# Queries and keys parted over 128 rows and placed by DMA, with forget sums, weight splits and fillers rearranged

## The chip, the cores and the metric

The kernel runs on one core of a Trainium2 chip. The metric is the time of one execution on the device in microseconds, the median of several runs. All times below are in us unless they are marked ns.

## The reference

Two layers (`DEPTH` 2) work on 512 tokens of width 1024. Each layer is a half-weighted SwiGLU block, a token mixer and a second SwiGLU block, with a layer norm behind each. The mixer projects once with `w_in`, runs three attentions of 8 heads each over heads of 64, gates their outputs and projects back:

```python
def _token_mix(h, w_in, ...):
    q_a, kv_a, g_a, q_b, k_b, v_b, q_c, k_c, v_c, f_c = _split_cols(h @ w_in)
    o_a = _nsa(q_a, kv_a, g_a, ...)      # compressed, selected and window keys, 2 groups
    o_b = _swa_sink(q_b, k_b, v_b, ...)  # window of 128, a sink in each row, 2 groups
    o_c = _fox(q_c, k_c, v_c, f_c, b_f)  # causal, with forget gates
    g = jax.nn.sigmoid(h @ w_gate + b_gate).reshape(B, S, 3, D)
    merged = g[:, :, 0] * (o_a @ w_br_a) + g[:, :, 1] * (o_b @ w_br_b) + g[:, :, 2] * (o_c @ w_br_c)
    return merged @ w_out

def _fox(q_c, k_c, v_c, f_c, b_f):
    log_f = jax.nn.log_sigmoid((f_c + b_f).astype(jnp.float32))
    c = jnp.cumsum(log_f, axis=1).transpose(0, 2, 1)
    ...
    logits = jnp.einsum('bhqd,bhkd->bhqk', qq, k) * scale
    logits = logits + cq[..., None] - c[:, :, None, :]
```

All of it is float32.

## The kernel before

**Products in three parts.** A float32 operand of a product is parted into a high part `hi` (a copy as fp32r) and a low part `lo` (the rest), and `mm3` runs three products: data high times weight high, data low times weight high, data high times weight low. For weights `wsplit` does it: ScalarE copies `raw` to `hi`, VectorE subtracts to `lo`. It does so in two operations of 512 columns each, or in one of 1024 where the pool `more` is open, which is outside of attention.

**One program per engine.** There are no loops on the chip. TensorE, VectorE, ScalarE, GpSimd (POOL) and SyncE (SP, which issues nearly all DMAs) each run a list of instructions in order, with semaphores between them. Tiles come from pools with a fixed number of buffers; a writer waits until the last reader of a buffer is done.

**The mixer, `mix(l, ...)`.** In attention all data lie transposed, the 128 partitions holding two heads of 64. `chunk(c0, then)` projects 128 columns of `w_in`: eight pieces of three products of 512 columns each, and after the eighth `then` takes the result out of PSUM. Chunks aren't run at once. Their pieces go into the list `fill`, and `pump(n)` takes n of them out. `step(cur, prev, n)` lays the scores of one batch of heads (`s`) and the transposes of the weights of the batch before (`tr`) on TensorE, and n pieces of `fill` between them; then the products with the values (`pv`) into `po`, which ScalarE copies to `o_t`. `PUMPS` lists n for each step. So the order of TensorE is written out by hand: projections fill the places in which a softmax on ScalarE and VectorE would leave TensorE without work. `last` holds two of the n pieces back for the end of the step. What attention is left with at its end, an empty step runs.

**Queries.** `ev_q` takes a query chunk (two heads) into `qs`, whose 128 rows hold for each head the high part in 64 rows and the low part in the other 64. For each head ScalarE writes the 64 high rows (L403) and VectorE the 64 low rows (L404).

**Keys.** `ev_k` parts the keys of a chunk in the same way, two operations on each engine (L414, L415), into `kh` and `kl`, each of which then needs its 64 rows a second time in the other 64. GpSimd copies them (L420), or VectorE for the first chunk.

**Order of the first chunks.** In each layer the mixer starts with the keys of the windowed heads (`CKB`), their first query, the columns of gates and forget gates (`set_gf`, 64 rows only), their second query, and `pump(29)`; behind these come `CKV + 0` and `CKV + P` (for `zk` and `zv`, the inputs of Nsa's compression), with a query between them, and then the rest.

**Forget sums.** `set_gf` puts two things into `fill`: at place 4 `late`, which transposes the gates and runs a chain of small operations on ScalarE and VectorE that ends with `f` (L465); at place 14 `m.cum`, which multiplies `f` by a triangle of ones on TensorE (`cum`, L475) and sends the sums through DRAM into the tables `nck`, which Fox reads.

**Gates.** `gate_chunk(br)` runs column block 0 of each branch's gates as fillers. One further chunk (branch 0, block 1) is run as a filler too, and its result stays in its PSUM bank in `held` until attention is over; `gates(1)` then takes it from there and computes the other two. `ps("mm")` draws on two PSUM banks, `ps()` without a tag takes the eight banks in turn.

**Names in the rows.** `pj` is a projection, `sS`, `sF`, `sN`, `sC` are scores of the windowed heads, Fox, Nsa and its compressed keys, `ptN` and `ptC` the transposed weights of Nsa, `p` and `pc` the weights themselves, `raw` a loaded weight.

Of the kernel before, what the change touches and what calls it, by code (L numbers as in the profile page):

```python
# [18 lines left out]
P = 128  # L19
S, D, F = 512, 1024, 2816  # L20
KD, KF, NB = D // P, F // P, S // P
H, DH, NSLOT = 8, 64, 32
# [42 lines left out]
def body(tc, a, out, depth=DEPTH):  # L65
    nc = tc.nc
# [49 lines left out]
    more = K()  # L116
# [12 lines left out]
    def wsplit(raw, n=KD, step=None):  # L129
        if nx.pool:  # L130
            pl, nb = nx.pool, 4
        else:
            more.n += 1
            pl, nb = (more.pool, 2) if more.pool and more.n % 5 in (4, 0) else (wt, 3)
        hi = pl.tile([P, KD, P], F32R, name="hi", tag="hi", bufs=nb)
        lo = pl.tile([P, KD, P], F32R, name="lo", tag="lo", bufs=nb)
        step = step or (n if more.pool else 4)
        for i in range(0, n, step):
            c = slice(i, i + step)
            nc.scalar.activation(hi[:, c], raw[:, c], AF.Copy)  # L140
            nc.vector.tensor_tensor(lo[:, c], raw[:, c], hi[:, c].bitcast(F32), op=OP.subtract)  # L141
        return hi, lo
# [208 lines left out]

    def mix(l, wts, pend, done_ffn, xap, xa, nxt):
        m = K()
        PB = 14
        w_in = a["w_in"][l]
        wb = [a["w_br_a"][l], a["w_br_b"][l], a["w_br_c"][l]]

# [7 lines left out]
        op = pool("op", side="right", reuse_waits="tile")  # L365
        o_t = [[op.tile([P, S], F32, name=f"o{br}{i}") for i in range(4)] for br in range(3)]
        at = pool("at", reuse_waits="tile")
# [27 lines left out]
                    nc.scalar.activation(dst, src, AF.Copy)  # L395


        def ev_q(p):

            t = at.tile([P, 2, S], F32R, name="qs", tag="qs", bufs=3)  # L400
            for s in range(2):
                h, o = slice(64 * s, 64 * s + 64), slice(64 - 64 * s, 128 - 64 * s)
                nc.scalar.activation(t[h, s], p[h], AF.Copy, scale=0.125)  # L403
                nc.vector.scalar_tensor_tensor(t[o, s], p[h], 0.125, t[h, s].bitcast(F32), op0=OP.mult,  # L404
                                               op1=OP.subtract)
            return t

        def ev_k(p, dst, first=False):

            for s in range(2):  # L410
                h, o = slice(64 * s, 64 * s + 64), slice(64 - 64 * s, 128 - 64 * s)
                kh, kl = dst(s)
                pv = p[h].rearrange("p (a b) -> p a b", b=P)
                nc.scalar.activation(kh[h], pv, AF.Copy)  # L414
                nc.vector.tensor_tensor(kl[h], pv, kh[h].bitcast(F32), op=OP.subtract)  # L415
                for x in (kh, kl):
                    if first:
                        nc.vector.tensor_copy(x[o], x[h].bitcast(F32))
                    else:
                        nc.gpsimd.tensor_scalar(x[o], x[h].bitcast(F32), 1.0, 1.0, op0=OP.mult, op1=OP.mult)  # L420

        def ks_tile():
            return at.tile([P, 8, P], F32R, name="ks", tag="ks", bufs=8)
# [14 lines left out]
        def ev_gf(p):  # L438
            t = at.tile([P, S], F32, name="vt", tag="vt", bufs=2)
            nc.scalar.activation(t[0:64], p[0:64], AF.Copy)  # L440

            def rest():
                pt = ps("tp", "gfT", (P, NB, 64))
                for tb in range(NB):
                    nc.tensor.transpose(pt[:, tb], t[0:64, tb * P:(tb + 1) * P], ident[0:64, 0:64])
                gs = at.tile([P, NB, 32], F32, name="gs")
                nc.scalar.activation(gs, pt[:, :, 0:32], AF.Copy)
                nc.vector.tensor_tensor(gs, gs, pt[:, :, 32:64], op=OP.add)
                nc.scalar.activation(gt, gs[:, :, 0:24], AF.Tanh, scale=0.5)
                nc.vector.tensor_scalar(gt, gt, 0.5, 0.5, op0=OP.mult, op1=OP.add)  # L450
                f = at.tile([P, 7, NB, H], F32, name="f")
                x, e, d, u, lu, eq, lf = [f[:, i] for i in range(7)]
                nc.vector.tensor_tensor(x, gs[:, :, 24:32], bf[:, None, :].to_broadcast([P, NB, H]), op=OP.add)
                nc.vector.scalar_tensor_tensor(e, x, -1.0, x, op0=OP.mult, op1=OP.min)
                nc.scalar.activation(e, e, AF.Exp)
                nc.vector.tensor_scalar(u, e, 1.0, None, op0=OP.add)
                nc.scalar.activation(lu, u, AF.Ln)
                nc.vector.tensor_scalar(d, u, -1.0, None, op0=OP.add)
                nc.vector.tensor_scalar(eq, d, 0.0, None, op0=OP.is_equal)
                nc.vector.tensor_tensor(d, d, eq, op=OP.add)  # L460
                nc.vector.reciprocal(d, d)
                nc.vector.tensor_tensor(lu, lu, d, op=OP.mult)
                nc.vector.tensor_tensor(lu, lu, eq, op=OP.add)
                nc.vector.tensor_tensor(lu, lu, e, op=OP.mult)
                nc.vector.scalar_tensor_tensor(lf, x, 0.0, lu, op0=OP.min, op1=OP.subtract)  # L465

                tri = at.tile([P, P], F32, name="tri", tag="pc", bufs=6)
                nc.gpsimd.affine_select(tri, ones.to_broadcast([P, P]), pattern=[[1, P]], compare_op=OP.is_ge,
                                        fill=0.0, base=0, channel_multiplier=-1)

                def cum():
                    pc = ps("tp", "cum")
                    for tb in range(NB):
                        c = tb * P
                        nc.tensor.matmul(pc[0:H, c:c + P], lf[:, tb], tri, start=tb == 0, stop=tb == NB - 1,  # L475
                                         skip_group_check=True)
# [113 lines left out]
        class Swa:  # L590
            br, nseg, ngrp = 1, 1, 1
# [53 lines left out]
        class Fox:  # L645
            br, nseg, ngrp = 2, 2, 2
# [4 lines left out]
            def s(u):  # L651
# [2 lines left out]
                kh, kl = m.kc[u.m]  # L654
                u.p = []
                st = small([P, 4, 2], "stF")
                for s in range(2):
                    p = p_tile([P, S])
                    u.p.append(p)
                    sc = ps("sc", "sF")  # L660
                    q = u.q[:, s, u.qb * P:(u.qb + 1) * P]
# [32 lines left out]
        class Nsa:  # L694
# [6 lines left out]
            def s(u):  # L701
# [21 lines left out]
                for s in range(2):  # L723
                    nc.scalar.activation(pc[:, s], pc[:, s], AF.Exp, scale=-1.0, bias=nm[:, 3 * s:3 * s + 1],
                                         accum_out=sm[:, 3 * s:3 * s + 1])
                u.p, u.n = [], []
                for s in range(2):
                    if s:
                        yield
                    pn = p_tile([P, 2, 2, P])[:, 0:near]  # L730
                    pf = p_tile([P, 2, 2, P])[:, 0:far] if far else None
                    u.p.append([pf[:, j] for j in range(far)] + [pn[:, j] for j in range(near)])
                    q = u.q[:, s, qb * P:(qb + 1) * P]
# [160 lines left out]

        def set_kb(p):
            m.kb = (ks_tile(), ks_tile())
            ev_k(p, lambda s: tuple(x[:, 4 * s:4 * s + 4] for x in m.kb), True)

        def set_gf(p):
            rest = ev_gf(p)  # L900

            def late():
                m.cum = rest()
            fill.insert(min(4, len(fill)), late)
            fill.insert(min(14, len(fill)), lambda: m.cum())


        chunk(CKB, set_kb)
# [4 lines left out]
        chunk(CKV + 0, lambda p: setattr(m, "zk", ev_z(p, 0)))  # L913
        chunk(CQB + 2 * P, set_q(m.qb, 2))
        chunk(CKV + P, lambda p: setattr(m, "zv", ev_z(p, 1)))
        cv, parts, tr = conv([a["cmp_k_w1"][l], a["cmp_v_w1"][l]])
        n0 = len(fill)
        chunk(CQB + 3 * P, set_q(m.qb, 3))
# [21 lines left out]
        held = []  # L940
# [6 lines left out]

        for br in range(3):
            gate_chunk(br)
        chunk(P, held.append, a["w_gate"][l])  # L950

        def need(u):
            if u.br == 1:
# [53 lines left out]
                for j, u in enumerate(prev):  # L1007
                    nc.scalar.activation(o_t[u.br][u.m][:, u.qb * P:(u.qb + 1) * P], po[:, j], AF.Copy)

        PUMPS = [11] * 8 + [10, 10, 12] * 4 + [8]  # L1010
        for cur, prev, n in zip(batches + [[]], [[]] + batches, PUMPS):
            step(cur, prev, n)
        while fill:
# [22 lines left out]
        def gates(d):  # L1036
            g_t = []
            for br in range(3):
                if d == 1 and br == 0:
                    p = held[0]  # L1040
                else:
                    p = ps(name="gate")
                    proj(p, wcols(a["w_gate"][l], br * D + d * P))
                t = tp_.tile([P, S], F32, name="t", tag="t", bufs=4)
                gate_ev(t, p, br, d)
                g_t.append(t)
            return g_t
# [163 lines left out]
```

## Time and profile before

| | |
|---|---|
| median of 3 runs | 2587.04 us (2584.88, 2587.04, 2588.99) |
| profiled execution | 2589.08 us, of which the span of the profile is 2587.4 |
| mean granted clock of TensorE | 0.996 |
| DMA | 256.39 MB, 99 GB/s in the mean |
| attention of layer 0, of layer 1 | about 415 to 714, 1697 to 1996 of the span |

The profiled execution is one more run, recorded by the hardware profiler; times within it are counted from the start of its span. Rows of groups give source line, engine, operation, tile out<-in, shape and count, then busy time and mean duration in ns, then the engine's idle time just before them with what ended most of it. Rows of waits give the waiting engine and tile, what released it, and sum, count and longest of the waits. Rows of the timeline give start, busy time, engine, line, operation, shape and count.

### The profile page before, as it was taken

The numbers are of one execution on the slowest core, as the hardware profiler recorded it, in microseconds if no ns is written. First come the engines' busy times: TensorE is split into PE (matmuls) and PEld (weight loads), VectorE is DVE, ScalarE is ACT, GpSimd is POOL, SyncE is SP. The second block draws the span as 40 slices with busy tenths as digits, with TensorE's granted clock in tenths as the row PEclk, the third lists the DMA queues.
The fourth block names the chain that finished last, engine by engine and source line by source line (L and its number), as shares of the span: only waits on it lengthen the run. The fifth ranks groups of instructions, "written<-read, shape, count | busy, mean of one in ns | idle before, by whom it ended". The sixth has DMA issues, their size and how long they took to land.

```text
span 2587.4 us, 34084 instructions
## 1 busy us (share of the span) xinstructions
PE 2558.4 (99%) x13099; PEld 2110.0 (82%) x13099; DVE 1212.7 (47%) x2633; ACT 960.9 (37%) x2015; POOL 210.9 (8%) x419
## 2 busy tenths in 40 slices
PE   9999999999999999999999999999999999999998
PEld 8888887788888888888888888877888888888887
DVE  4444244677654354442344432556766434533323
ACT  3222223577733232222232221345777323322211
POOL 0000000244300000000000000002432000000000
PEclk9999999999999999999999999999999999999999
DMA  6333333421143433333333332424221534233331
GB/s 214 110 96 98 98 92 102 138 73 52 46 140 89 125 107 96 95 96 96 114 90 95 96 96 97 127 71 138 62 59 34 151 98 142 83 98 98 98 91 64
DMA packets 360835, 256.39 MB, mean 99 GB/s; under 512 B 15336, under 2 KB 341032, under 8 KB 360672
## 3 DMA queue, kind: packets, MB, share of 16 engines
q1 hardware_dynamic: 359520, 250.02, 32.7%
q0 software_dynamic: 1152, 4.19, 0.4%
q8 instruction: 103, 1.69, 0.3%
q14 instruction: 60, 0.49, 0.1%
HBM read 247.83 MB, written 9.49 MB: 99 GB/s over the span
## 4 chain that ended last, share of the span: by engine, by line
PE 93%; DVE 4%; ACT 2%; issue 1%; DMA 0%; POOL 0%; POOLq 0%; DVEq 0%; ACTq 0%
PE acc L176 7%; PE acc L174 7%; PE acc L175 7%; PE pg L161 6%; PE pg L163 6%; PE pg L162 6%; PE pu L163 6%; PE pu L162 6%; PE pu L161 6%; PE pj L161 4%; PE pj L163 4%; PE pj L162 4%; PE gate L161 3%; PE gate L163 3%; PE gate L162 3%; PE brp L161 2%
## 5 line engine op out<-in xcount | busy, mean ns | idle before, releaser
L141 DVE TENSOR_TENSOR lo<-raw,hi 128x1024 fp32r<-128x1024 f32 (+2 forms) x470 | 500.9, 1074 | 853.5 <-ACT hi L140 852.3
L140 ACT ACTIVATE hi<-raw 128x1024 fp32r<-128x1024 f32 (+2 forms) x470 | 430.6, 930 | 1224.7 <-issue 707.3
L161 PE MATMUL pj<-xh,hi 128*128 128x512 f32 (+1 forms) x704 | 265.1, 377 | 0.8 <-DVE qs L404 0.7
L161 PE MATMUL pg<-xh,hi 128*128 128x512 f32 x640 | 249.9, 390 | 0.0
L163 PE MATMUL pj<-xh,lo 128*128 128x512 f32 (+1 forms) x704 | 249.4, 354 | 0.3 <-DVE lo L141 0.3
L162 PE MATMUL pj<-xl,hi 128*128 128x512 f32 (+1 forms) x704 | 248.7, 353 | 0.9 <-DVE xl L221 0.9
L162 PE MATMUL pg<-xl,hi 128*128 128x512 f32 x640 | 249.5, 390 | 0.0
L163 PE MATMUL pg<-xh,lo 128*128 128x512 f32 x640 | 249.5, 390 | 0.0
L163 PE MATMUL pu<-xh,lo 128*128 128x512 f32 x640 | 249.0, 389 | 0.0
L161 PE MATMUL pu<-xh,hi 128*128 128x512 f32 x640 | 249.0, 389 | 0.0
L162 PE MATMUL pu<-xl,hi 128*128 128x512 f32 x640 | 249.0, 389 | 0.0
L174 PE MATMUL acc<-hi,ha 128*128 128x512 f32 x576 | 227.3, 395 | 0.0
L175 PE MATMUL acc<-hi,ha 128*128 128x512 f32 x576 | 227.3, 395 | 0.0
L176 PE MATMUL acc<-lo,ha 128*128 128x512 f32 x576 | 227.2, 395 | 0.0
L203 POOL TENSOR_SCALAR st<-st 128x1 f32<-128x1 f32 x24 | 6.3, 264 | 1903.1 <-ACT junk L201 1903.1
L286 DVE TENSOR_TENSOR t<-t,pu 128x512 f32<-128x512 f32 x80 | 55.0, 687 | 216.6 <-PE pu L163 216.6
L161 PEld LDWEIGHTS pj<-xh,hi 128*128 128x128 f32 x704 | 134.0, 190 | 21.3 <-issue 7.2
L163 PEld LDWEIGHTS pj<-xh,lo 128*128 128x128 f32 x704 | 133.0, 189 | 19.8 <-DVE lo L141 0.5
L162 PEld LDWEIGHTS pj<-xl,hi 128*128 128x128 f32 x704 | 133.8, 190 | 11.5 <-DVE xl L221 1.6
L162 PEld LDWEIGHTS pg<-xl,hi 128*128 128x128 f32 x640 | 120.6, 188 | 25.1
L161 PEld LDWEIGHTS pg<-xh,hi 128*128 128x128 f32 x640 | 120.5, 188 | 25.1
L163 PEld LDWEIGHTS pg<-xh,lo 128*128 128x128 f32 x640 | 120.5, 188 | 25.0
(243 smaller groups left out, 4417.6 us busy)
## 6 DMA issues: line engine op xcount, KB each, us to landing
raw<-in_ffn_w_dram SPq DMA_DIRECT2D x264, 512.0 KB, 3.8
raw<-in_w_in_dram SPq DMA_DIRECT2D x56, 512.0 KB, 4.1
raw<-in_w_gate_dram SPq DMA_DIRECT2D x48, 512.0 KB, 4.0
raw<-in_w_out_dram SPq DMA_DIRECT2D x16, 512.0 KB, 3.5
x_sp<-xa POOLq DMA_DIRECT2D x8, 512.0 KB, 6.6
tab<-bvec SPq DMA_DIRECT2D x16, 256.0 KB, 2.8
raw<-in_cmp_k_w_dram SPq DMA_DIRECT2D x16, 256.0 KB, 2.7
raw<-in_cmp_v_w_dram SPq DMA_DIRECT2D x16, 256.0 KB, 3.3
```

The source lines that it names most:

```text
L140: nc.scalar.activation(hi[:, c], raw[:, c], AF.Copy)
L141: nc.vector.tensor_tensor(lo[:, c], raw[:, c], hi[:, c].bitcast(F32), op=OP.subtract)
L161: nc.tensor.matmul(o, hi[:, k], vh, start=first, stop=False)
L162: nc.tensor.matmul(o, hi[:, k], vl, start=False, stop=False)
L163: nc.tensor.matmul(o, lo[:, k], vh, start=False, stop=last)
L174: nc.tensor.matmul(o, sh(k)[:, t], hi[:, c], start=k == 0, stop=False)
L175: nc.tensor.matmul(o, sl(k)[:, t], hi[:, c], start=False, stop=False)
L176: nc.tensor.matmul(o, sh(k)[:, t], lo[:, c], start=False, stop=k == nk - 1)
L203: nc.gpsimd.tensor_scalar(st[:, 4:5], st[:, 3:4], 1.0 / D, EPS / ALPHA ** 2, op0=OP.mult, op1=OP.add)
L286: nc.vector.tensor_tensor(t, t, pu, op=OP.mult)
```

## The change

- `wsplit` parts a weight in one operation on each engine everywhere.
- A new `hi_lo` parts all 128 rows of a query or key chunk in one operation on ScalarE and one on VectorE, into two tiles `hl`. `ev_q` then places the four blocks of 64 rows in `qs` by four DMAs, `ev_k` the eight blocks (each part twice) in `kh` and `kl` by eight DMAs, all issued by SP. GpSimd's copies go.
- `m.cum` is appended to `fill` behind the chunk `CKV + P`.
- Two gate chunks are held instead of one. `PUMPS` deals the pieces in another way: 11 x 5, 12 x 3, then 11, 10, 11 four times, then 8.
- Some tiles share buffers: `p` has 13 instead of 14, the forget gates' scratch comes from the same buffers, and small pairs of `p` tiles become one.

```diff
-        step = step or (n if more.pool else 4)
+        step = step or n
...
-        PB = 14
+        PB = 13
...
+        def hi_lo(p, scale):
+            hi, lo = [at.tile([P, S], F32R, name="hl", tag="hl", bufs=2) for _ in range(2)]
+            nc.scalar.activation(hi, p, AF.Copy, scale=scale)
+            nc.vector.scalar_tensor_tensor(lo, p, scale, hi.bitcast(F32), op0=OP.mult, op1=OP.subtract)
+            return hi, lo
         def ev_q(p):
             t = at.tile([P, 2, S], F32R, name="qs", tag="qs", bufs=3)
-            for s in range(2):
-                h, o = slice(64 * s, 64 * s + 64), slice(64 - 64 * s, 128 - 64 * s)
-                nc.scalar.activation(t[h, s], p[h], AF.Copy, scale=0.125)
-                nc.vector.scalar_tensor_tensor(t[o, s], p[h], 0.125, t[h, s].bitcast(F32), op0=OP.mult,
-                                               op1=OP.subtract)
+            for o, x in zip((slice(0, 64), slice(64, P)), hi_lo(p, 0.125)):
+                for s in range(2):
+                    nc.sync.dma_start(t[o, s].bitcast(F32), x[64 * s:64 * s + 64].bitcast(F32))
             return t
-        def ev_k(p, dst, first=False):
-            for s in range(2):
-                ...
-                nc.scalar.activation(kh[h], pv, AF.Copy)
-                nc.vector.tensor_tensor(kl[h], pv, kh[h].bitcast(F32), op=OP.subtract)
-                for x in (kh, kl):
-                    if first:
-                        nc.vector.tensor_copy(x[o], x[h].bitcast(F32))
-                    else:
-                        nc.gpsimd.tensor_scalar(x[o], x[h].bitcast(F32), 1.0, 1.0, op0=OP.mult, op1=OP.mult)
+        def ev_k(p, dst):
+            for i, x in enumerate(hi_lo(p, 1.0)):
+                for s in range(2):
+                    k = dst(s)[i]
+                    v = x[64 * s:64 * s + 64].bitcast(F32).rearrange("p (a b) -> p a b", b=P)
+                    for o in (slice(0, 64), slice(64, P)):
+                        nc.sync.dma_start(k[o].bitcast(F32), v)
...
-            fill.insert(min(14, len(fill)), lambda: m.cum())
...
         chunk(CKV + P, lambda p: setattr(m, "zv", ev_z(p, 1)))
+        fill.append(lambda: m.cum())
...
-        chunk(P, held.append, a["w_gate"][l])
+        for br in range(2):
+            chunk(br * D + P, held.append, a["w_gate"][l])
...
-        PUMPS = [11] * 8 + [10, 10, 12] * 4 + [8]
+        PUMPS = [11] * 5 + [12] * 3 + [11, 10, 11] * 4 + [8]
...
-                if d == 1 and br == 0:
-                    p = held[0]
+                if d == 1 and br < 2:
+                    p = held[br]
```

More of the change, by code (lines that the diff above doesn't have):

```diff
@@ L395, in ev_pt @@
                     nc.scalar.activation(dst, src, AF.Copy)
+        def hi_lo(p, scale):
[3 more added lines that the diff above has]
+            return hi, lo
         def ev_q(p):
             t = at.tile([P, 2, S], F32R, name="qs", tag="qs", bufs=3)
-            for s in range(2):
-                h, o = slice(64 * s, 64 * s + 64), slice(64 - 64 * s, 128 - 64 * s)
-                nc.scalar.activation(t[h, s], p[h], AF.Copy, scale=0.125)
-                nc.vector.scalar_tensor_tensor(t[o, s], p[h], 0.125, t[h, s].bitcast(F32), op0=OP.mult,
-                                               op1=OP.subtract)
-            return t
-        def ev_k(p, dst, first=False):
-            for s in range(2):
-                h, o = slice(64 * s, 64 * s + 64), slice(64 - 64 * s, 128 - 64 * s)
-                kh, kl = dst(s)
-                pv = p[h].rearrange("p (a b) -> p a b", b=P)
-                nc.scalar.activation(kh[h], pv, AF.Copy)
-                nc.vector.tensor_tensor(kl[h], pv, kh[h].bitcast(F32), op=OP.subtract)
-                for x in (kh, kl):
-                    if first:
-                        nc.vector.tensor_copy(x[o], x[h].bitcast(F32))
-                    else:
-                        nc.gpsimd.tensor_scalar(x[o], x[h].bitcast(F32), 1.0, 1.0, op0=OP.mult, op1=OP.mult)
+            for o, x in zip((slice(0, 64), slice(64, P)), hi_lo(p, 0.125)):
+                for s in range(2):
+                    nc.sync.dma_start(t[o, s].bitcast(F32), x[64 * s:64 * s + 64].bitcast(F32))
+            return t
+        def ev_k(p, dst):
[5 more added lines that the diff above has]
+                        nc.sync.dma_start(k[o].bitcast(F32), v)
         def ks_tile():
@@ L445, in rest @@
                     nc.tensor.transpose(pt[:, tb], t[0:64, tb * P:(tb + 1) * P], ident[0:64, 0:64])
-                gs = at.tile([P, NB, 32], F32, name="gs")
+                w = at.tile([P, 11, NB, H], F32, name="gl", tag="p", bufs=PB)
+                gs = w[:, 0:4].rearrange("p a b h -> p (a b h)").rearrange("p (b c) -> p b c", b=NB)
                 nc.scalar.activation(gs, pt[:, :, 0:32], AF.Copy)
@@ L450, in rest @@
                 nc.vector.tensor_scalar(gt, gt, 0.5, 0.5, op0=OP.mult, op1=OP.add)
-                f = at.tile([P, 7, NB, H], F32, name="f")
-                x, e, d, u, lu, eq, lf = [f[:, i] for i in range(7)]
+                x, e, d, u, lu, eq, lf = [w[:, 4 + i] for i in range(7)]
                 nc.vector.tensor_tensor(x, gs[:, :, 24:32], bf[:, None, :].to_broadcast([P, NB, H]), op=OP.add)
@@ L656, in s @@
                 st = small([P, 4, 2], "stF")
+                both = p_tile([P, 2, 256]) if nk <= 256 else None
                 for s in range(2):
-                    p = p_tile([P, S])
+                    p = both[:, s] if both is not None else p_tile([P, S])
                     u.p.append(p)
@@ L726, in s @@
                 u.p, u.n = [], []
+                both = p_tile([P, 2, 2, P]) if near == 1 else None
                 for s in range(2):
@@ L729, in s @@
                         yield
-                    pn = p_tile([P, 2, 2, P])[:, 0:near]
+                    pn = both[:, s:s + 1] if near == 1 else p_tile([P, 2, 2, P])
                     pf = p_tile([P, 2, 2, P])[:, 0:far] if far else None
@@ L896, in set_kb @@
             m.kb = (ks_tile(), ks_tile())
-            ev_k(p, lambda s: tuple(x[:, 4 * s:4 * s + 4] for x in m.kb), True)
+            ev_k(p, lambda s: tuple(x[:, 4 * s:4 * s + 4] for x in m.kb))
         def set_gf(p):
```

## The prediction

> **What bounds the kernel now.** First the page, then TensorE's waits, then its instructions where the waits are.
>
> ```profile
> span 2587.4 us, 34084 instructions
> PE 2558.4 (99%) x13099; PEld 2110.0 (82%) x13099; DVE 1212.7 (47%) x2633; ACT 960.9 (37%) x2015; POOL 210.9 (8%) x419
> ```
>
> TensorE is busy for 2558.4 of 2587.4 us, and no edit takes a product from it. So all that there is to win lies in 29 us of idle time, and in time in which it is busy at less than its clock. The waits say where the idle time is:
>
> ```profile
> PE cum L475 <- DVE f L465: 7.2, 2, 3.6
> PE xT L1154 <- DMA xa<-in_x_dram: 5.0, 1, 5.0
> PE ptN L783 <- ACT p L395: 1.3, 2, 0.7
> PE ptN L783 <- DVE p L393: 1.2, 2, 0.6
> PE ptC L789 <- ACT p L395: 1.2, 2, 0.6
> PE ptC L789 <- DVE p L393: 1.0, 2, 0.5
> PE ptN L783 <- DVE pc L393: 0.7, 2, 0.3
> PE pj L161 <- DVE qs L404: 0.7, 2, 0.3
> ```
>
> The columns are the sum, the number and the longest. The largest is the forget sums (`cum`), once in each layer. Here it is in layer 0 and in layer 1, on TensorE alone (start, busy time, line, operation, count, and in brackets the wait before it):
>
> ```profile
> 435.13 0.59 PE L475 MATMUL cum<-tri,f 128*8 128x128 f32 x2 [3.60 <-DVE f L465]
> 439.48 0.80 PE L161 MATMUL pj<-xh,hi 128*128 128x512 f32 x1
> 441.20 0.40 PE L162 MATMUL pj<-xl,hi 128*128 128x512 f32 x1
> 441.44 0.39 PE L163 MATMUL pj<-xh,lo 128*128 128x512 f32 x1
> ```
>
> ```profile
> 1717.39 0.42 PE L475 MATMUL cum<-tri,f 128*8 128x128 f32 x2 [3.60 <-DVE f L465]
> 1721.33 0.50 PE L161 MATMUL pj<-xh,hi 128*128 128x512 f32 x1
> 1721.67 0.39 PE L162 MATMUL pj<-xl,hi 128*128 128x512 f32 x1
> ```
>
> And by windows, a quiet one and the two of the sums (busy us of PE and of the other engines, then granted clock, DMA share and GB/s):
>
> ```profile
> 418.00:420.00 2.00, 2.00 (x10) 1.64 (x10) 1.44 (x3) 0.00 (x0) 0.00 (x0) 1.00 0.88 249
> 435.10:439.40 4.30, 4.27 (x14) 1.71 (x14) 1.37 (x4) 1.39 (x6) 0.57 (x1) 0.50 0.34 118
> 1717.40:1721.30 3.90, 3.90 (x14) 1.63 (x14) 1.37 (x4) 1.36 (x5) 0.57 (x1) 0.56 0.37 125
> ```
>
> After 3.60 us without work the sums run at a granted clock of 0.50 and 0.56, and the projections behind them start at it too. The wait costs more than its idle time.
>
> The Trainium skill ("TensorE: Matmul & The Clock Gate", section "HAM oscillation — how this bites in real kernels") says that gaps of TensorE beyond about 3.4 us let the clock fall to half. The two gaps of 3.60 us agree.
>
> **The sums placed later (a gain).** They move behind the projection chunk that feeds `zv`, three chunks further; their input `f` is done at the moment where TensorE stops waiting, 435.1, so it is long there. Layer 0: 3.60 us idle; the sums take 439.48 − 435.13 = 4.35 us at 0.50, so 2.2 at full clock, a saving of 2.2; the next four products take 441.20 − 439.48 = 1.72 where four at the later spacing (441.44 − 441.20 = 0.24) take 0.9, a saving of 0.8. That is 6.6. Layer 1: 3.60; 1721.33 − 1717.39 = 3.94 at 0.56 against 2.2, a saving of 1.7; the first product's 0.34 instead of 0.24, 0.1. That is 5.4. Together **−12.0 us**. What reads the sums, the table for Fox, is first used some 80 us later, so nothing is late behind them. The softmax of the first windowed heads, which the gap sheltered, has seven fill pieces before its transposes in the new order.
>
> **Queries and keys (off the path in their arithmetic, on it in their landing).** The costs of the operations, by their groups in the attention of layer 0:
>
> ```profile
> L403 ACT ACTIVATE qs<-pj 64x512 fp32r<-64x512 f32 x24 | 14.1, 588 | 8.7 <-DVE qs L404 7.1 <-PE pj L163 1.4
> L427 ACT ACTIVATE vt<-pj 128x512 f32<-128x512 f32 x3 | 1.7, 579 | 0.0
> L404 DVE SCALAR_TENSOR_TENSOR qs<-pj,qs 64x512 fp32r<-64x512 f32 x24 | 16.5, 688 | 5.5 <-ACT qs L403 5.1
> ```
>
> An operation over 128 rows (579 ns) takes what one over 64 does (588), so each of 12 query and 7 key chunks of a layer loses one ScalarE and one VectorE operation: 19 x 0.588 = 11 and 19 x 0.688 = 13 us a layer, and GpSimd its copies of keys. None of them bounds (DVE 47% busy, ACT 37%), so this is worth nothing by itself; what it frees is the PSUM bank, one pair of operations earlier, and with it the 0.7 us of `pj` on `qs`: **−0.7**.
>
> In their place come 4 DMAs for each query chunk and 8 for each key chunk, 104 a layer, of 128 KB, all on SP's queue, in order with the weight loads. No DMA from SBUF to SBUF is in this trace; the nearest:
>
> ```profile
> raw<-in_w_in_dram SPq DMA_DIRECT2D x56, 512.0 KB, 4.1
> raw<-in_cmp_k_w_dram SPq DMA_DIRECT2D x16, 256.0 KB, 2.7
> raw<-in_cmp_v_w_dram SPq DMA_DIRECT2D x16, 256.0 KB, 3.3
> x_sp<-xa POOLq DMA_DIRECT2D x8, 512.0 KB, 6.6
> ```
>
> ```profile
> 433.67 0.37 SPq L518 DMA_DIRECT2D raw<-in_cmp_k_w_dram  x1
> 434.09 0.46 SPq L518 DMA_DIRECT2D raw<-in_cmp_v_w_dram  x1
> ```
>
> So SP issues one every 0.42 us, 44 us of a layer's 300, and a small load lands 2.7 us after its issue; 6.6 is the far end. Keys, and the queries of Fox and of the later windowed heads, are read 12 us or more after their chunk by the order of TensorE's instructions, so these hide it. Two kinds do not.
>
> The first query chunk, read 7 us after its end:
>
> ```profile
> 420.08 0.40 PE L158 MATMUL pj<-xh,hi 128*64 128x512 f32 x1
> 420.10 1.16 ACT L140 ACTIVATE hi<-raw 128x512 fp32r<-128x512 f32 x2 [2.31 <-PE pj L162]
> 427.60 0.66 PE L607 MATMUL sS<-ks,qs 128*128 128x128 f32 x4
> ```
>
> (Without its wait on `qs`, 0.3 in the waits above, the last row is 427.2.) ScalarE first splits a weight (until 421.2), then the query (0.588, 421.8); VectorE follows with the weight (an estimate: as long as ScalarE's 1.16, 422.4) and the query (0.688, 423.1). SP's order there is: eight key DMAs, two of the query's high part, two weight loads, two of the low part. At 0.42 each from 421.8 the weights go out at 422.6 and 423.1 and the last low part at 423.9. Alone it lands 2.7 later, 426.6: no wait. Served strictly behind the weights it is: the first weight at 422.6 + 4.1 = 426.7, the second 2.1 later (512 KB at the 249 GB/s of the first window), the low part's 256 KB 1.05 later, 429.8: a wait of 2.6. I take the middle, 1.3 a layer: **+2.6**, ends 0 and 5.2.
>
> The Trainium skill ("DMA: Bandwidth & Descriptors", section "Queues, rings and completion order") says that each DMA engine takes the descriptors of one ring in order; by that alone this term would be its upper end, 5.2, and the whole sum 2.6 us worse. The trace leans that way (the second of a pair of 256 KB loads takes 3.3 against 2.7).
>
> The four query chunks of Nsa, read soon after their end:
>
> ```profile
> 521.95 0.57 ACT L403 ACTIVATE qs<-pj 64x512 fp32r<-64x512 f32 x1
> 523.08 0.37 SPq L147 DMA_DIRECT2D raw<-in_w_in_dram  x1
> 526.48 0.30 PE L714 MATMUL sC<-kc,qs 128*128 128x64 f32 x2
> ```
>
> From the chunk's end to the read are 4.4 us in this one (526.48 less 521.95, and ScalarE starts at once). By the order of instructions 1.0 us of products more lie between them in the new kernel, and 1.8, 3.1 and 2.4 at the other three: 5.4 us of room at the tightest, and 4.4 + 2.1 = 6.5 in the mean (an estimate that gives all four this one's room). The second low part is issued about 2.4 us after the chunk's end: 0.6 for ScalarE, some 0.7 in VectorE's queue, 0.7 for its operation, 0.4 on SP. Landing after 2.7 it is there at 5.1, in time; behind a weight load issued at the same moment, as at 523.08, it lands as late as that one, in 4.1, 1.4 later, and the tightest waits 1.1. I take 0.8 a layer, **+1.6**; ends 0 and 5 (0.6 for each of the eight).
>
> SP's order also puts four query DMAs between the loads of the compression weights, whose buffers turn over in a few us: 0.3 a layer, **+0.6**, ends 0 and 2.
>
> **Weights split in one operation.** The pair of half splits takes 1.16 us on ScalarE (420.10 above); as one operation its first half comes up to 0.6 later and its second no later. A chunk's weights are made two chunks ahead; no wait of the list above is on `hi` or `lo`. Nothing, unless another operation comes to wait 0.5 us longer behind one on VectorE: inside the next term.
>
> **Fillers and the held gate.** In the last step eight projection pieces now stand between the transposes, where before two did:
>
> ```profile
> 709.18 0.30 PE L789 MATMUL ptC<-ident,pc 128*128 128x128 f32 x1 [0.49 <-DVE p L393]
> 710.42 0.66 PE L783 MATMUL ptN<-ident,p 128*128 128x128 f32 x4 [0.33 <-DVE pc L393]
> 713.99 0.50 PE L161 MATMUL gate<-xh,hi 128*128 128x512 f32 x1
> 714.14 0.45 ACT L1008 ACTIVATE o<-po 128x128 f32<-128x128 f32 x2 [2.38 <-PE po L802]
> 714.47 0.69 ACT L943 ACTIVATE t<-pj,bgate 128x512 f32<-128x512 f32 x1
> ```
>
> Those two waits go in both layers: **−1.6**. But a new one comes. Both `mm` banks are now held, and the next gate takes the bank of the first: in layer 0 its first product waits for ScalarE's copies of `po` and the tanh behind them, from 713.99 until 714.47 + 0.69 = 715.2: 1.2. One call fewer in the ring of banks makes it the bank of `po` in layer 1: 0.6. **+1.8.** Of the other waits of `ptN` and `ptC` (5.4 in the rows above, less 1.6: 3.8) more products lie ahead of some and VectorE has 10% less to do; I take half, **−1.9**, ends 0 and −3.8.
>
> **The sum.** −12.0 − 0.7 + 2.6 + 1.6 + 0.6 − 1.6 + 1.8 − 1.9 = **−9.6 us**; the ends give −16.3 and −0.3. The profiled execution took 2589.08 (its span and 1.7 around it), so 2579.5; the median of the runs lies 2.0 below it, 2587.04, so **2577**.
>
> **Rivals.** *Slower: the placed halves land late.* It stands against the change that no such DMA is in the trace, that x_sp takes 6.6 us, and that DMAs of 128 KB need the whole of SP's turn; for it that 256 KB loads land in 2.7. With landing L the first scores wait 423.9 + L − 427.2 = L − 3.3 a layer, the four Nsa queries, with room of 6.5 and 2.4 until the issue, L − 4.1 each. All else sums to −13.8, 6.9 a layer, so it decides from 5L − 19.7 = 6.9: L = 5.3. At the far row, 6.6, it is 2 x (3.3 + 10.0) − 13.8 = +12.8: 2600. Chance 0.14.
>
> *No change: the gap comes back at the first scores.* If the low part of the first query lands 3.4 us late in both layers, TensorE idles as long as before and the clock falls: 3.5 + 2.4 a layer instead of 1.3, +9.2 over the forecast: 2586. It needs the queue above and a further 0.8 us, as from VectorE being busy. Chance 0.12.
>
> *The remaining idle time goes too*: all fillers fit, nothing waits on a DMA: 2587 − 16.3 = 2571. Chance 0.12. The forecast itself has 0.62.
>
> **How the numbers follow.** About 0.2%, 5.2 us, is what a measurement of this kernel can tell from no change. The forecast is over that in nine cases of ten, the third rival always, the second seldom: faster 0.69, same 0.16, slower 0.15. The range leaves out the rest of the first rival and the far end of the third: 2569 to 2591, which is the first rival up to L = 5.7.
>
> **What would show it.** Right: no wait of `cum`; granted clock 1.0 through the attention of both layers; `cum` in about 2.2 us; waits of `sS` on the DMA of `qs` of 0 to 2.6 us, twice; a wait of `gate` on ScalarE of about 1.2 in layer 0; an idle sum of about 22 us. Wrong: a wait of `sC` on `qs` of over 1 us each, `qs` DMAs landing after 4.7 us, or a stretch at clock 0.5 behind the first scores.

## The result, and the profile after

The changed kernel takes 2600.47 us (median of 4 runs, 2596.84 to 2601.57) against 2586.96 for the kernel before: 1.005 times as long, 95% interval 1.0032 to 1.0067. Faster was forecast, 2577 in a range of 2569 to 2591; it is slower by 13.5 us, what the first rival priced at 2600.

The profiled execution took 2601.57, its span 2599.9, 12.5 more than before. The page, busy times first:

```profile
span 2599.9 us, 34236 instructions
PE 2561.5 (99%) x13099; PEld 2112.6 (81%) x13099; DVE 1175.3 (45%) x2529; ACT 933.8 (36%) x1923; POOL 177.6 (7%) x371
```

DVE, ACT and POOL lose 37, 27 and 33 us of work, as the change means them to. TensorE's idle time rises from 29.0 to 38.4, and the same products keep it busy 3.1 us longer. The waits of TensorE (sum, number, longest) say where:

```profile
PE sC L715 <- DMA qs<-hl: 6.6, 6, 1.8
PE sS L607 <- DMA qs<-hl: 4.2, 2, 3.9
PE kv L560 <- DMA cw2k<-in_cmp_k_w_dram: 4.2, 2, 2.2
PE sS L607 <- issue: 2.7, 1, 2.7
PE ptC L791 <- ACT p L395: 1.5, 2, 0.7
PE sC L715 <- DVE stF L675: 1.4, 1, 1.4
PE gate L161 <- ACT t L945: 1.1, 1, 1.1
PE gate L161 <- ACT o L1011: 0.5, 1, 0.5
```

The waits of `cum` and of `pj` on `qs` are gone, those of `ptN` and `ptC` shrink from 5.4 to 1.5. In their place stand the scores of the windowed heads (`sS`, 6.9 in all) and of Nsa's compressed keys (`sC`, 8.0), both on the placed queries, and `kv`, the second product of the compression, on its weights (4.2). Two of these rows don't name the placed queries (`sS` on issue, `sC` on `stF`); they are counted to them for their place and because they disappear when all placing goes back to the engines (below).

The sums themselves went as planned. By windows (PE's busy time, then the other engines, granted clock, DMA share, GB/s), the sums of layer 0 and layer 1 in their new place:

```profile
457.00:460.50 3.50, 3.50 (x22) 2.00 (x21) 1.88 (x6) 1.67 (x6) 0.00 (x0) 1.00 0.29 60
1747.00:1750.50 3.50, 3.50 (x22) 2.05 (x21) 1.88 (x6) 1.67 (x6) 0.00 (x0) 1.00 0.21 68
```

No gap, and full clock. But a gap of the same length opened at the first scores of layer 0. TensorE there, and SP's issues ahead of it (start and time on the queue):

```profile
431.04 1.06 PE L607 MATMUL sS<-ks,qs 128*128 128x128 f32 x4 [3.90 <-DMA qs<-hl]
431.90 0.73 PE L161 MATMUL pj<-xh,hi 128*128 128x512 f32 x1
432.43 0.63 PE L162 MATMUL pj<-xl,hi 128*128 128x512 f32 x1
```

```profile
416.07 5.01 SPq L420 DMA_DIRECT2D ks<-hl  x8
421.59 1.10 SPq L410 DMA_DIRECT2D qs<-hl  x2
422.74 1.34 SPq L147 DMA_DIRECT2D raw<-in_w_in_dram  x2
424.18 1.47 SPq L410 DMA_DIRECT2D qs<-hl  x2
426.68 0.37 SPq L518 DMA_DIRECT2D raw<-in_cmp_k_w_dram  x1
427.10 0.46 SPq L518 DMA_DIRECT2D raw<-in_cmp_v_w_dram  x1
```

The order is the predicted one: eight key DMAs, high parts, two weights, low parts. The eight keys hold SP for 5.01 us, 0.63 each. The low parts go out at 424.18 and 425.06 and land 6.73 and 6.37 us later by their records, at 430.91 and 431.43; `sS` starts at 431.04 with the first of its four. What lies between is a full set of DMA engines:

```profile
427.00:428.00 1.00, 0.14 (x3) 0.01 (x1) 0.47 (x2) 0.47 (x2) 0.00 (x0) 1.00 1.15 295
429.00:430.00 1.00, 0.00 (x0) 0.00 (x0) 0.00 (x0) 0.99 (x2) 0.00 (x0) 1.00 1.07 252
431.00:435.30 4.30, 4.15 (x12) 3.33 (x13) 2.27 (x16) 1.30 (x6) 0.76 (x2) 0.60 0.02 6
1721.93:1725.35 3.42, 3.42 (x10) 2.65 (x10) 2.27 (x16) 1.34 (x6) 0.76 (x2) 0.50 0.02 7
```

The busy share of the 16 DMA engines reads above 1 while the low parts are on their way. And behind the gap the clock falls to half: the product at 432.43 takes 0.63 us where one at full clock takes 0.39, and the granted clock is 0.60 in the mean over 4.3 us. Layer 1 shows the same (last row): `sS` starts after a gap of 2.75 us, and 1.1 us later the clock goes to half for 3.4 us.

To add both kinds of loss, I took for each product the time to the next start beyond the usual one for its number of columns (the median of the kernel before), and summed it by place, over both layers:

| place | before | after | forecast of the difference |
|---|---|---|---|
| forget sums | 13.5 | 1.7 | −12.0 |
| first scores, `sS` | 0 | 11.0 | +2.6 |
| scores of Nsa's queries, `sC` | 0 | 12.9 | +1.6 |
| compression, `kv` | 0 | 7.9 | 0 (its loads +0.6) |
| first gate behind attention | 0 | 2.2 | +1.8 |
| whole kernel | 14.6 | 27.2 | −9.6 |

The whole differs by 12.6, as the spans do. What the rows of the table leave out (transposes, `pj`, and small differences in the usual spacing) is −9.6 by difference; that this is also the number of the forecast is chance. Of the 31.8 us of `sS`, `sC` and `kv`, some 7.6 lie in five stretches at half clock, the rest is idle time.

### The profile page after: what moved, and what is told of

Same layout as the page of the kernel before. It is cut to its first block, busy times and chain, and to the rows that moved or that the text cites. A ratio compares the mean times of both kernels' runs of the same rounds, so it can differ in the third digit from the quotient of the medians.

```text
span 2599.9 us, 34236 instructions
## 1 busy us (share of the span) xinstructions
PE 2561.5 (99%) x13099; PEld 2112.6 (81%) x13099; DVE 1175.3 (45%) x2529; ACT 933.8 (36%) x1923; POOL 177.6 (7%) x371
## 5 line engine op out<-in xcount | busy, mean ns | idle before, releaser
L141 DVE TENSOR_TENSOR lo<-raw,hi 128x1024 fp32r<-128x1024 f32 (+2 forms) x414 | 490.6, 1189 | 867.4 <-ACT hi L140 867.3
L140 ACT ACTIVATE hi<-raw 128x1024 fp32r<-128x1024 f32 (+2 forms) x414 | 424.4, 1031 | 1247.0 <-issue 709.2
L161 PE MATMUL pj<-xh,hi 128*128 128x512 f32 (+1 forms) x720 | 274.8, 382 | 0.1
L163 PE MATMUL pj<-xh,lo 128*128 128x512 f32 (+1 forms) x720 | 257.5, 358 | 1.1 <-DVE lo L141 0.9
L162 PE MATMUL pj<-xl,hi 128*128 128x512 f32 (+1 forms) x720 | 256.6, 356 | 1.3 <-DVE xl L221 1.3
L161 PEld LDWEIGHTS pj<-xh,hi 128*128 128x128 f32 x720 | 137.8, 191 | 19.1 <-issue 6.6
L161 PEld LDWEIGHTS pu<-xh,hi 128*128 128x128 f32 x640 | 120.2, 188 | 25.0
```

Source lines behind the costliest of these rows:

```text
L161: nc.tensor.matmul(o, hi[:, k], vh, start=first, stop=False)
L162: nc.tensor.matmul(o, hi[:, k], vl, start=False, stop=False)
L163: nc.tensor.matmul(o, lo[:, k], vh, start=False, stop=last)
```

## The experiments

All times are medians; ratios are to the kernel before on the same chip, with 95% intervals.

**All placing back on the engines.** `ev_q` and `ev_k` as before, everything else changed.

```diff
-        def hi_lo, ev_q, ev_k ...      # shortened: by DMA
+        def ev_q, ev_k ...             # shortened: as in the kernel before
```

> The changed kernel with its queries and keys parted and placed as before (64 rows at a time on ScalarE and VectorE, second copies of keys by GpSimd); all else of the change stays. Theory A (the placed halves land late): the waits of sS on qs (11.0 us with the half clock behind them), of sC on qs (12.9) and of kv on the compression weights behind the key DMAs (7.9) go, 31.8 in all; pj on qs (1.2) comes back: 2600.5 - 30.6 = 2570. Theory B (the arrangement of fillers and held gates costs it, and the waits on qs only stand where others would): the transposes and the first scores wait for the softmax instead, and it stays at 2587 or above. In A TensorE's idle sum is about 20 us, in B 30 or more.

2572.50 us, 0.9945 (0.9933 to 0.9958). Theory A holds: the placing costs the changed kernel 28 us (forecast 30.6), and everything else of the change gains 14. Its waits:

```profile
PE ptC L791 <- ACT p L395: 1.5, 2, 0.7
PE pj L161 <- ACT vt L440: 1.4, 2, 0.7
PE pj L163 <- DVE lo L141: 1.1, 2, 0.8
PE gate L161 <- ACT t L945: 1.1, 1, 1.1
```

No `sS`, `sC` or `kv` is left, and the transposes wait about as long as in the changed kernel (`ptC` 1.5 in both, `ptF` 1.1 against 0.4), which speaks against theory B. TensorE's idle sum is 20.5 us, as theory A had it.

**Queries alone and keys alone by DMA.** Each is the changed kernel with one of the two functions of before.

> The changed kernel with its keys as before, its queries still by DMA. Theory A, by parts: the wait of kv goes (7.9 us with the clock), since the eight key DMAs ahead of the compression weights are gone; the waits of sC stay (12.9) and that of sS mostly (the weight loads still stand ahead of the low half): 2592, between 2588 and 2594. If the number of DMAs on SP's queue is what makes all of them late (104 a layer become 48), the waits on qs shrink too, and it is 2580 or below.

> The changed kernel with its queries as before, its keys still by DMA. Theory A, by parts: the waits of sS and sC on qs go (23.9 us), pj on qs comes back (1.2), the wait of kv stays (7.9): 2578, between 2575 and 2582. If the keys' DMAs are themselves late for scores, sS, sF or sN wait on ks instead, and it is above 2585.

With the keys on the engines: 2582.20, 0.9984 (0.9976 to 0.9993). With the queries on the engines: 2573.09, 0.9947 (0.9935 to 0.9960). Both forecasts by parts are too high, by 10 and 5 us: the parts don't add, and the first run comes near the other reading, by the number of DMAs on SP's queue (2580 or below), without reaching it. Against 2572.5, queries alone by DMA cost 9.7, keys alone 0.6, both 28. The rows of the first:

```profile
PE sC L720 <- DMA qs<-hl: 2.9, 7, 1.1
PE sS L612 <- DMA qs<-hl: 2.7, 2, 1.5
PE sC L720 <- DVE stF L680: 1.1, 1, 1.1
```

and of the second:

```profile
PE kv L562 <- DMA cw2k<-in_cmp_k_w_dram: 2.3, 2, 1.2
```

So no product waits for a placed key (no such row in any run). The keys' DMAs are harmful by what they do to others: to the queries and to the compression's weights.

**Which keys.** The changed kernel with the first chunk's keys, or Nsa's two chunks, on the engines.

```diff
-            ev_k(p, lambda s: tuple(x[:, 4 * s:4 * s + 4] for x in m.kb))
+            ev_k_of_before(p, lambda s: ..., True)      # first chunk; in the other run nsa_k's call
```

> The changed kernel with only the keys of the first chunk as before (their eight DMAs in each layer gone); all other keys and all queries by DMA. Theory A: those eight DMAs, 5.0 us of SP's time right ahead, push the two weight loads behind them into the path of the first query's low half. Without them the low half lands as in the kernel with all keys on the engines (idle 2.7 us in both layers instead of 6.7, without a clock at half): 11.0 us become some 3, and it is 2600.5 - 8 = 2592.5. Rival: the low half is late because it follows weight loads on its queue however early they are: sS keeps 10 us or more, 2600.

> The changed kernel with only Nsa's two key chunks as before (sixteen DMAs of a layer gone). Theory A: the compression weights are issued and land in time, kv's wait goes with the clock at half behind it (7.9), and the first of Nsa's queries, right behind the second chunk's eight DMAs, waits less (4.3 us in both layers with the clock): 2600.5 - 7.9 - 1 to 3 = 2590 to 2592. Rival: kv waits for weights that are late for another reason (the Fox keys' DMAs, which stand ahead of them too): 2597 or above.

First chunk: 2587.43, 1.0005 (0.9996 to 1.0014). Nsa's: 2593.34, 1.0031 (1.0021 to 1.0042). The rows of the two:

```profile
PE sS L621 <- DMA qs<-hl: 2.6, 2, 1.6
PE kv L574 <- DMA cw2k<-in_cmp_k_w_dram: 4.2, 2, 3.2
PE sC L729 <- DMA qs<-hl: 3.3, 3, 1.5
```

```profile
PE sS L621 <- DMA qs<-hl: 4.1, 2, 3.9
PE kv L574 <- DMA cw2k<-in_cmp_k_w_dram: 3.1, 2, 1.8
PE sC L729 <- DMA qs<-hl: 4.5, 7, 2.0
```

Without the eight first DMAs, `sS` waits 2.6 instead of 6.9 and the clock stays at 1.00 there. One of the two weight loads now goes out at 416.6, long before the query. The other still goes out right ahead of the low parts, at 422.76, and these land 4.8 and 4.4 us after their issue instead of 6.7 and 6.4. By windows:

```profile
415.00:435.00 20.00, 18.41 (x87) 14.19 (x86) 12.03 (x36) 10.26 (x20) 0.71 (x2) 1.00 0.41 105
```

In the changed kernel this stretch reads 15.99 us busy, clock 0.92 and a share of 0.65. The rival (late however early the loads are) falls. The run gained 13.0, not 8: `sC` waits less too, and why the first chunk's keys touch that is not shown. Nsa's keys gained 7.1 by the median (its runs lie between 2591.4 and 2600.4) where 9 to 11 were forecast; `kv` still waits 3.1 instead of 4.2, so Nsa's own key DMAs are only part of its cause, as its rival said.

**Other queues.** The changed kernel with the placing DMAs issued by another engine.

```diff
-                    nc.sync.dma_start(t[o, s].bitcast(F32), ...)      # and in ev_k
+                    nc.scalar.dma_start(...)                          # or nc.gpsimd
```

> The changed kernel with all its placing DMAs issued by ScalarE, on ScalarE's own DMA queue, instead of by SP between the weight loads. Theory A (what makes the halves late is that they stand in one queue behind weight loads, and that SP is issuing for 89 us of a layer's 300): a half lands in about 2.3 us, as the key DMAs with no load ahead of them do, the waits of sS, sC and kv on DMAs shrink from 17 us of idle time to under 5; ScalarE takes over some 60 us of issuing a layer and waits for VectorE's low parts, so that some transposes come to wait for the softmax: 2575 to 2590. Theory B (SBUF to SBUF transfers share the DMA engines with the weights and are slow beside them, whatever the queue): the low halves land in 4.5 to 6.7 us still and it stays at 2595 or above.

> The changed kernel with its placing DMAs issued by GpSimd. The transfers from GpSimd's queue in the traces (x_sp) land 5.3 to 6.6 us after their issue. Theory A: the halves are off SP's queue, so kv's wait goes (7.9 with the clock), but a landing of 5 us or more makes the waits of sS and sC as long as they are: 2590 to 2605. If the halves land in under 3 us from this queue too, the waits go and it is 2575 to 2580.

ScalarE: 2600.19, 1.0051 (1.0035 to 1.0066). GpSimd: 2631.86, 1.0176 (1.0162 to 1.0190). Theory A failed in both: ScalarE's time is where theory B put it (2595 or above), GpSimd's lies 27 us above the upper end of its range. The groups of DMAs (KB each, median us to landing), of the changed kernel and then of ScalarE's queue:

```profile
ks<-hl SPq DMA_DIRECT2D x112, 128.0 KB, 2.5
qs<-hl SPq DMA_DIRECT2D x96, 128.0 KB, 3.2
raw<-in_w_in_dram SPq DMA_DIRECT2D x56, 512.0 KB, 4.3
```

```profile
ks<-hl ACTq DMA_DIRECT2D x112, 128.0 KB, 4.6
qs<-hl ACTq DMA_DIRECT2D x96, 128.0 KB, 3.5
```

A queue of their own doesn't make them faster. Sorting the placed halves whose landing is recorded by whether SP issued a weight load (256 or 512 KB) in the 2 us ahead (median us to landing, number):

| kernel | none ahead | one or more ahead |
|---|---|---|
| changed, queries on SP | 2.7 (21) | 4.5 (9), 6.7 (1 with two ahead) |
| queries on ScalarE's queue | 3.0 (21) | 4.6 (6), 4.9 (2) |
| queries on GpSimd's queue | 2.7 (55) | 4.7 (27), 4.2 (14) |
| keys on ScalarE's queue | 4.2 (18) | 5.2 (10) |
| keys on GpSimd's queue | 3.8 (69) | 5.1 (43) |

A half with one weight load just ahead lands 1.0 to 2.1 us later, on every queue, though the loads stand on SP's. The bytes count: behind two loads of 512 KB a half took 6.7 us on SP (6.8 and 7.0 in two other runs) and 6.9 on GpSimd's queue, one record each; most of the 4.2 on GpSimd's are behind two of 256 KB. So the delay goes with the loads and not with the queue in which the half stands, which points to the DMA engines, read as full above. No run changed their load alone. The Trainium skill ("DMA: Bandwidth & Descriptors", section "Queues, rings and completion order") says of the first two that SP's and ScalarE's queues are rings on the same engines and not engines of their own; this table agrees. On ScalarE the issuing disturbs its own order besides: its operation for the next query, behind eight key DMAs, sat idle for them,

```profile
423.35 0.60 ACT L401 ACTIVATE hl<-pj 128x512 fp32r<-128x512 f32 x1 [7.58 <-DMA ks<-hl]
```

since the two `hl` buffers were still being read. There `sS` no longer waits on `qs`, but TensorE waits for a PSUM bank that VectorE's part of `hl` still reads (3.6), at `sC` (6.1) and at `kv` (6.4): the time is that of the changed kernel, the waits are others. On GpSimd `sC` alone waits 21.4 us: GpSimd issues in order and idles ahead of the placing DMAs for ScalarE's part (91.5 us in all) and VectorE's (19.1), with its scaling of weights behind them.

**The sums alone.** The kernel before with `m.cum` moved.

> The kernel before with nothing but the forget sums moved behind the chunk for zv. The prediction's first term alone: the 3.6 us gap and the half clock behind it go in both layers, 2587 - 12 = 2575 (2574 to 2577), granted clock 1.0 there. Rival: the first scores' softmax, sheltered by the gap before, is now waited for at its transposes (ptS), up to 3.6 us a layer: 2582 or above.

2575.92, 0.9961 (0.9947 to 0.9974), 10.3 us less. The first term of the prediction was right; no `ptS` waits.

**The placing alone.** The kernel before with `ev_q` and `ev_k` by DMA.

```diff
-        PB = 14
+        PB = 12                        # and hi_lo, ev_q, ev_k of the changed kernel
```

> The kernel before with nothing but the placing by DMA (and two buffers fewer for p, to have the room). Theory A: the waits of sC and kv add (12.9 + 7.9); that of sS stands ahead of the forget sums, whose chain goes on meanwhile, so the two overlap and the larger is paid (11.0 for 13.5): 2586 + 20.8 = 2607, between 2603 and 2610. If they do not overlap, all of the 28 us that the placing costs in the changed kernel come on top: 2614.

2624.44 (2616.86 to 2628.16), 1.0143 (1.0127 to 1.0158): more than either theory gave. The profile is that of the fastest run. It shows the overlap that theory A expected, for only one of `sS` and `cum` is waited for,

```profile
PE sC L714 <- DMA qs<-hl: 10.4, 9, 2.3
PE kv L560 <- DMA cw2k<-in_cmp_k_w_dram: 7.8, 2, 3.9
PE sS L607 <- DMA qs<-hl: 6.8, 3, 4.1
```

and `sC` and `kv` wait longer than in the changed kernel (8.0 and 4.2). Whether the two buffers fewer for `p` or the other order of fillers does that wasn't separated.

**Fillers and gates.** The kernel with all placing on the engines, once with one held gate and the fillers of before, once with the third gate of block 1 in a bank of the scores.

```diff
-                    p = ps(name="gate")
+                    p = ps("sc" if d == 1 else None, name="gate")
```

> The changed kernel with queries and keys parted and placed as before, one held gate and the fillers dealt as before: what is left of the change is the late sums, the weights split in one operation and the shared buffers. If these two are worth nothing, it has the time of the late sums alone, 2576, and the 3.4 us between that and 2572.5 belong to the fillers and the second held gate; if the weight splits in one operation are what ended the waits of ptN and ptC (some 7 us of them are gone), it is 2572 to 2573.

> The changed kernel with queries and keys parted and placed as before, and the third gate of column block 1 taking a PSUM bank of the scores instead of the bank of the first held gate. The first gate products behind attention then wait for nothing: without the 1.1 and 0.5 us of idle time (2.2 with the clock) it is 2572.5 - 2 = 2570 to 2571. If another wait of the same end (the table load of the tanh, po) stands behind it, 2572.

Old fillers: 2577.53, 0.9968 (0.9955 to 0.9980). So the new dealing and the second held gate are worth 5.0 us, and weights split in one operation with the shared buffers nothing that can be told (2577.5 against 2575.9 of the sums alone, intervals overlapping). The other bank: 2571.28, 0.9939 (0.9927 to 0.9952), 1.2 us less; the intervals don't tell the two apart, but no `gate` row is left.

**What can be kept of the placing.** Queries on the engines, keys by DMA, the compression's second weights loaded with the step ahead of Nsa's keys, and the gate's bank.

```diff
             def tr():
+                wk, wv = ...; nc.sync.dma_start(wk[:, :, r], v); nc.sync.dma_start(wv, ...)
                 pt = ps("tp", "glT", (P, 2, P))
```

> The changed kernel with queries as before and keys by DMA, the compression's second weights loaded one step earlier, ahead of Nsa's key DMAs, and the third gate of block 1 in a bank of the scores. Without kv's wait (2.3 us of idle time) and the gates' (1.2 by the run with the other bank) it is 2573.1 - 3.5 = 2569.5; if the GpSimd copies and second operations that the key DMAs replace are worth anything, it is below the version with all on the engines and the gate's bank (2571.3), otherwise within 1 us of it.

2566.01 (2565.44 to 2568.88), 0.9923 (0.9909 to 0.9936): by its median faster than every other version here. Its largest waits inside attention:

```profile
PE ptC L795 <- ACT p L395: 1.5, 2, 0.7
PE pj L161 <- ACT vt L442: 1.4, 2, 0.7
```

`kv` is gone by loading 192 KB a step earlier. The median is 5.3 us below the version with all placing on the engines and the gate's bank, with intervals that just overlap. Part of it is chance: in the profiled execution of that version the clock is at half for 3.4 us from 41.0 on, ahead of everything in which the two differ, and in this one it is not (this run first):

```profile
38.00:46.00 8.00, 8.00 (x37) 5.74 (x37) 4.26 (x8) 1.62 (x3) 0.00 (x0) 1.00 0.61 171
38.00:46.00 8.00, 8.00 (x31) 5.57 (x31) 4.18 (x8) 1.35 (x2) 0.00 (x0) 0.79 0.56 159
```

By the start of the 301st product this run is 1.9 us ahead (49.3 against 51.2); what follows is 3.2 us shorter. With nothing late behind them, the keys' DMAs seem to bring that much; by what is not shown.

## Why the prediction was wrong, point by point

**Right.** The bound: TensorE's idle time and its clock, nothing else. The late sums: −12.0 forecast, −11.8 by the table and −10.3 as an edit alone (medians). `cum` takes 2.3 us from first start to next product (457.36 to 459.63 in the timeline), 2.2 forecast. The held gate: +1.8 forecast, 1.6 of idle time. `pj` on `qs`: gone. Transposes: −3.5 forecast, 5.4 to 1.5, −3.9. Parting over 128 rows and weights in one operation are worth nothing by themselves. All this is the 14 us that the kernel gains without the placing.

**Wrong: the landing of the placed queries.** This is the step that failed, and three sizes were off in it. SP's issue was taken as 0.42 us from loads from DRAM; a placing DMA holds SP for 0.59 in the median (`ks` 461 to 1391 ns, `qs` 461 to 1636). The last low half was to go out at 423.9 and went at 425.06. Its landing was taken as the middle between 2.7 and "behind the weights"; it was beyond the end, 431.43 against 429.8; two further loads of 256 KB, which the estimate left out, went out meanwhile (426.68 and 427.10); whether they delayed it is not shown. And each gap was priced at its idle time alone, though the first part of the prediction had just shown that a gap of 3.6 us costs the clock too. Together: first scores +11.0 for +2.6 (end 5.2), Nsa's queries +12.9 for +1.6 (end 5). The sentence that the trace "leans that way", on the second of a pair of loads, was the evidence at hand, and taking the middle set it aside. The rule on the order of a ring, cited there, pointed the right way, but the runs don't need it: on a queue without the loads the halves are as late behind them. One reading was off without changing anything: from 521.95 to 526.48 are 4.5 us, not 4.4.

**Wrong: what the key DMAs delay.** They were costed by their own reader, which indeed never waits. Their place ahead of others on SP (weights, query halves, the compression's `cw2k`) was listed for the first query only: `kv` was not looked at, +7.9. Queries alone by DMA cost 9.7 and keys alone 0.6; the 18 on top are the two in each other's way.

**The rivals.** The first rival had the mechanism and the break-even: landing decides from 5.3, and the recorded landings with loads ahead are 4.5 to 6.7. Its 2600 is met, in part by chance, since `kv` and the clock are not in its sum. The second rival's picture, the gap and the half clock returning at the first scores, is what both layers show (3.90 and 2.75 us, each with 3.4 us at half clock behind it); its 2586 left out Nsa's queries and `kv`. With 0.14 and 0.12 both were given too little against the row of 3.3 us and 512 KB loads beside them.

## What to carry to other kernels

A DMA that replaces cheap work on an idle engine is priced by its landing while the weight stream runs, not alone: here 4.5 us instead of 2.7, and a gap of TensorE of some 2 us can cost its clock as well (here some 1.5 us more). Cost a moved transfer by everything that is issued behind it on its queue, not only by its own reader; and place such transfers where the first use is far (the keys, 12 us), leaving the near ones (the queries) on the engines. When a change has several parts, the parts that free the bound should be tried without the part that loads a queue: here 14 us of gain were under 28 of cost.

## What the runs showed of the hardware

The clock fell behind gaps much shorter than the 3.60 us of before. In the changed kernel, by TensorE's rows and windows:

```profile
672.34 0.59 PE L715 MATMUL sC<-kc,qs 128*128 128x64 f32 x2 [1.77 <-DMA qs<-hl]
531.85 0.55 PE L715 MATMUL sC<-kc,qs 128*128 128x64 f32 x2 [1.80 <-DMA qs<-hl]
```

After 1.77 us idle the clock fell to half, after 1.80 us it did not. The record shows what parts them. The five stretches at half clock in this kernel's attention begin at 431.70, 506.79, 674.04, 1721.93 and 1797.03, last 3.41 us each, and lie 22, 49, 307 and 22 times 3.413 us apart. So in this trace the clock changes on a fixed grid of 3.413 us. Cut on it (layout of the windows above):

```profile
670.63:674.04 3.41, 1.65 (x10) 1.42 (x11) 1.17 (x11) 1.56 (x7) 0.46 (x2) 1.00 0.04 11
674.04:677.46 3.42, 3.42 (x16) 3.02 (x14) 1.86 (x11) 2.50 (x12) 0.00 (x0) 0.50 0.00 0
527.26:530.68 3.42, 2.79 (x15) 2.06 (x13) 1.02 (x7) 1.43 (x6) 0.01 (x1) 1.00 0.99 237
530.68:534.09 3.41, 2.23 (x12) 1.91 (x13) 1.24 (x12) 0.88 (x5) 0.46 (x2) 1.00 0.03 6
534.09:537.50 3.41, 3.41 (x21) 2.96 (x20) 2.91 (x16) 3.29 (x11) 0.00 (x0) 1.00 0.40 93
```

The gap of 1.77 lies whole in one step, 1.76 us of it idle, and the next step runs at 0.50. The gap of 1.80 is parted over two, 0.63 and 1.18, and the clock stays. In this trace the steps ahead of half clock hold 1.76 to 2.87 us of idle time, the others of attention 1.51 or less; over the attention of all runs a step at full clock with under 1.58 us was never followed by half clock and one with over 1.87 always, with both kinds between. The gaps of 2.18 and 1.99 ahead of `kv` lie whole in one step each and were followed by 0.50. So the rule of the Trainium skill that the prediction used, gaps beyond about 3.4 us ("TensorE: Matmul & The Clock Gate", section "HAM oscillation — how this bites in real kernels"), is no safe limit here: about half of that was enough where it fell into one step. The stretch at half clock near 40 us, which differs between executions, stands behind no such gap; its cause is open.

A DMA of 128 KB from SBUF to SBUF lands in 2.2 us at the shortest and 2.5 to 3.2 in the median on SP, about as the loads of 256 KB from DRAM before (2.7 and 3.3), but holds its issuing engine longer: 0.59 in the median on SP, 0.61 and 0.56 on ScalarE, 0.52 on GpSimd, against 0.37 to 0.47 for a load before.
